# Two q tiles of a head pair share one item, and one pair of banks, in the prompt's attention

## The chip, the cores and the metric

The kernel runs on one core of one Trainium2 chip. The metric is device time in microseconds (us) for one execution, as the median of several runs; lower is better. A profiled execution of the same kernel gives the rows shown below.

## The reference, cut to what matters

The reference is one step of an encoder with two layers (each a mixer and a SwiGLU network, with RMS norms before and after) for 512 prompt frames and 8 running streams of 16 new frames each. The change lies in the attention of the second layer's mixer, and there in the prompt's part: 8 heads of 64 channels, 512 queries and 512 keys, each 64-frame chunk seeing itself and all chunks before it, with a relative-position bias:

```python
scores = einsum('bcqhd,bckhd->bchqk', chunks(q), kb) * 64 ** -0.5 + bias
probs = softmax(where(kpos >= 0, scores, -1e30), axis=-1)
out = einsum('bchqk,bckhd->bqhd', probs, vb)
```

The running streams' attention (the samples) reads 512 cached rows of keys and values for each of the 8 streams.

## The kernel before

All matrix products run on TensorE (PE) with weights split by ScalarE (ACT) and VectorE (DVE) into a coarse and a residual part (`split`, line 228), so that three fast products stand for one. The attention itself is computed in plain fp32.

The program is written by generators that a small planner, `Weave` (lines 48 to 84), takes turns with. The planner keeps a clock of its own: every matrix product adds an estimate (`mm`, line 164: columns divided by 2.4, in ns, four times as much for fp32, over `share` where products run side by side, plus 2 ns; `flip`, line 169, is a transpose on PE for 109 ns). A generator gives back control with `yield x`, which means "not before x nanoseconds from now", or with an event. Of the generators that are due, the one with the lowest priority number goes on, and of equals the one spawned first. The main line of the kernel has priority 9, so it fills what the others leave. The order that results is the program order; the instructions are then placed on the engines in nearly that order, but one whose inputs are reckoned to be late can be passed by a later one that is ready.

In the second layer's mixer, `odd_mixer` (line 933), the main line makes for each pair of heads j (0 to 3) the transposed keys and queries (`kq_proj`, line 1055), in products of 12 at a time: 48 of 256 columns and 48 of 384 columns for a pair. After each pair it signals `kq_ev[j]`. After the fourth pair it signals `room` and goes on with the first output chunk (`out_chunk`, line 437), whose products of 512 columns fill the time while the attention ends.

Three streams run beside it at priority 1 (line 1231). Two of them take items of the prompt from one shared list (line 1221): an item is a pair j and a q tile qt of 128 queries, with n = 128 (qt + 1) keys. An item takes two PSUM banks (one for each head), and does this:

- scores: two products side by side in the two halves of PE's rows (line 1094);
- for each head the bias is added and the maximum taken by DVE, the exponential and its sum made by ACT (lines 1098 to 1107); then DVE normalises the probabilities (line 1112);
- `yield 2200 + 5 * n`, a due time for the softmax;
- qt + 1 transposes for each head, back into the same bank, and a copy by ACT to SBUF (lines 1114 to 1118);
- `yield 600 + 1.5 * n`, then the products with the values into the bank `pos[j]` of the pair (line 1123). The fourth item of a pair splits that bank into an operand tile.

Once the list of the prompt is empty, the two streams take samples like the third one (`sample_stream`, line 1151). A sample loads 2 MB of cached keys and values in four transfers on the SP queue (`load`, line 1142). The first two samples' rows are loaded early; those of samples 2 to 7 go into the tiles of pool `xpool`, seven in all, of which five come free in this stage: four held the mixer's input, and one (`both`, line 921) holds the bias and is freed by the last item's bias additions. Later loads wait for the scores and value products of earlier samples.

The pool of PSUM banks has eight; an output chunk takes two, a pair's result one, each stream two.

Of the kernel before, what the change touches and what calls it, by code (L numbers as in the profile page):

```python
# [10 lines left out]
AF = mybir.ActivationFunctionType  # L11
ALU = mybir.AluOpType
AX = mybir.AxisListType

P = 128
D = 1024
NK = D // P
NP = 512
# [87 lines left out]
def trunk_kernel(  # L106
# [42 lines left out]
    act, dve = Ordered(tc, nc.scalar), Ordered(tc, nc.vector)  # L149
# [14 lines left out]
    def mm(out, lhsT, rhs, start, stop, n, share=1, more=False):  # L164
        fast = lhsT.dtype == F32R
        W.now += PASS * (max(n, 256) if fast else 4 * n / share) + 2
        nc.tensor.matmul(out, lhsT=lhsT, rhs=rhs, start=start, stop=stop, skip_group_check=more)  # L167

    def flip(out, in_):
        W.now += 109  # L170
        nc.tensor.transpose(out=out, in_=in_, identity=ident)  # L171
# [3 lines left out]
    def nm(s):  # L175
        uid[0] += 1
        return f"{s}{uid[0]}"

    def bank(shape=(P, 512)):
        return psp.tile(list(shape), F32, tag="ps", name=nm("ps"))  # L180
# [4 lines left out]
    def t2(shape):  # L185
        return t2p.tile(list(shape), F32, tag="t2", name=nm("t2_"))

    def st(n=1):
        return stp.tile([P, n], F32, tag="st", name=nm("st"))
# [38 lines left out]
    def split(dst, val):  # L228
        act.copy(out=dst[0], in_=val)
        dve.tensor_tensor(out=dst[1], in0=val, in1=dst[0].bitcast(F32), op=ALU.subtract)  # L230
# [202 lines left out]
    def hid_tile():  # L433
        return hidp.tile([P, 2, NT], F32R, tag="hid", name=nm("hid"))
# [466 lines left out]
    def bias_tables():  # L901
        fscr = drp.tile([P, 8, 384], F32, name="fscr")
        for hh in range(2):
            rev = t4([P, 4, 129])
            hs = slice(4 * hh, 4 * hh + 4)
            nc.sync.dma_start(out=rev, in_=rb_rev[0, hs, :].partition_broadcast(P))
            f = x10([P, 4, 384])
            nc.gpsimd.memset(f[:, :, 0:191], 0.0)
            dve.tensor_tensor(
                out=f[:, :, 191:320], in0=rev, in1=rev[:, :, 0:1].broadcast_to([P, 4, 129]), op=ALU.subtract  # L910
            )
            dve.tensor_copy(out=f[:, :, 320:384], in_=f[:, :, 319:320].broadcast_to([P, 4, 64]))
            nc.sync.dma_start(out=fscr[:, hs, :], in_=f)
        a = fscr[:, :, :]

        def skew(h, nh, q, n):
            return bass.AP(
                tensor=a.tensor, offset=a.offset + h * 384 + 127, ap=[[8 * 384 - 1, q], [384, nh], [1, n]]
            )

        both = x10([P, 2, 4, 256])
        bias = []
        for hh in range(2):
            b = both[:, hh]
            nc.sync.dma_start(out=b, in_=skew(4 * hh, 4, P, 256))
            nc.gpsimd.memset(b[0:64, :, 192:256], NEG)
            bias.append(b)
        bias_s = cst.tile([P, 144], F32, name="bias_s")
        for h in range(8):
            nc.sync.dma_start(out=bias_s[h * LS : (h + 1) * LS, :], in_=skew(h, 1, LS, 144)[:, 0, :])  # L930
        return bias, bias_s

    def odd_mixer(X):
# [13 lines left out]
        def vt(t):  # L947
            return vts[:, t, :]
# [81 lines left out]
        bias, bias_s = bias_tables()  # L1030
# [7 lines left out]
        done = [0] * 4  # L1038
# [5 lines left out]
        def row_max(parts):  # L1044
            m = st()
            if len(parts) == 1:
                dve.tensor_reduce(out=m, in_=parts[0], axis=AX.X, op=ALU.max, negate=True)
            else:
                m2 = st(2)
                for i, p in enumerate(parts):  # L1050
                    dve.tensor_reduce(out=m2[:, i : i + 1], in_=p, axis=AX.X, op=ALU.max)
                dve.tensor_reduce(out=m, in_=m2, axis=AX.X, op=ALU.max, negate=True)
            return m
# [29 lines left out]
        def prompt_stream(items):  # L1083


            for j, qt in items:
                yield kq_ev[j]
                kT, qT = kq[j]
                n = (qt + 1) * P
                nb_ = min(n, 256)  # L1090
                ss = [bank() for _ in range(2)]
                for h in range(2):
                    r = slice(64 * h, 64 * h + 64)
                    mm(ss[h][:, :n], qT[r, qt * P : (qt + 1) * P], kT[r, :n], True, True, n, 2)
                prs = []
                for h in range(2):
                    s, hd = ss[h], 2 * j + h
                    dve.tensor_tensor(
                        out=s[:, n - nb_ : n],
                        in0=s[:, n - nb_ : n],  # L1100
                        in1=bias[hd // 4][:, hd % 4, 256 - nb_ :],
                        op=ALU.add,
                    )
                    m = row_max([s[:, :n]])
                    pr = t2([P, NP])
                    sm = st()
                    act.activation(out=pr[:, :n], in_=s[:, :n], func=AF.Exp, bias=m, accum_out=sm)
                    prs.append((pr, sm))
                for pr, sm in prs:
                    ri = st()  # L1110
                    dve.reciprocal(out=ri, in_=sm)
                    dve.tensor_scalar(out=pr[:, :n], in0=pr[:, :n], scalar1=ri, scalar2=None, op0=ALU.mult)
                yield 2200 + 5 * n
                for h in range(2):
                    s, pr = ss[h], prs[h][0]
                    for kt in range(qt + 1):
                        flip(s[:, kt * P : (kt + 1) * P], pr[:, kt * P : (kt + 1) * P])
                    act.copy(out=pr[:, :n], in_=s[:, :n])
                yield 600 + 1.5 * n
                if j not in pos:  # L1120
                    pos[j] = bank()
                po = pos[j]
                for kt in range(qt + 1):
                    for h in range(2):
                        hd = 2 * j + h
                        mm(
                            po[64 * h : 64 * h + 64, qt * P : (qt + 1) * P],
                            vt(kt)[:, hd * 64 : hd * 64 + 64],
                            prs[h][0][:, kt * P : (kt + 1) * P],
                            kt == 0,  # L1130
                            kt == qt,
                            P,
                            2,
                        )
                done[j] += 1
                if done[j] == 4:
                    ct = cat[4 + j] = hid_tile()
                    split((ct[:, 0, :NP], ct[:, 1, :NP]), po)
                    W.signal(prompt_done[j], 2000)
                yield  # L1140
# [77 lines left out]
                    W.signal(sample_done, 500)  # L1218
                yield

        prompt_items = iter([(j, qt) for j in range(4) for qt in range(4)])
        sample_items = iter(range(NB))
        room = Event()

        def stream(i):
            if i < 2:
                yield from prompt_stream(prompt_items)
            yield room
            yield from sample_stream(sample_items)
# [34 lines left out]
    def main():  # L1264
# [39 lines left out]

        yield from ffn(0, X, mid)
        X = yield from odd_mixer(nxt[0])

        def end():
# [101 lines left out]
```

## Time and profile before

| | us |
|---|---|
| median of 3 runs | 1320.69 |
| lowest and highest | 1320.46, 1320.77 |
| profiled execution, its own time | 1320.24 |
| its span, first to last instruction | 1318.5 |
| PE busy | 1294.0 |
| DVE busy | 889.0 |
| ACT busy | 614.0 |

The span is what the profile's rows lie in; 1.7 us of the profiled execution's time lie around it. A busy time is the time in which an engine had an instruction under way; the ends of PE's products are modelled and overlap the next one's start, so that the cost of a block of products is best read as the distance between its start and the start of the next block.

### The profile page before, as it was taken

The numbers are of one execution on the slowest core, as the hardware profiler recorded it, in microseconds if no ns is written. First come the engines' busy times: TensorE is split into PE (matmuls) and PEld (weight loads), VectorE is DVE, ScalarE is ACT, GpSimd is POOL, SyncE is SP. The second block draws the span as 40 slices with busy tenths as digits, with TensorE's granted clock in tenths as the row PEclk, the third lists the DMA queues.
The fourth block names the chain that finished last, engine by engine and source line by source line (L and its number), as shares of the span: only waits on it lengthen the run. The fifth ranks groups of instructions, "written<-read, shape, count | busy, mean of one in ns | idle before, by whom it ended". The sixth has DMA issues, their size and how long they took to land.

```text
span 1318.5 us, 20069 instructions
## 1 busy us (share of the span) xinstructions
PE 1294.0 (98%) x8060; PEld 1178.4 (89%) x8060; DVE 889.0 (67%) x1452; ACT 614.0 (47%) x1130; POOL 54.9 (4%) x107
## 2 busy tenths in 40 slices
PE   6999999999999999999999999999999999999997
PEld 5998989989899998998799885789999898998996
DVE  6985779837576675776736556489557575864766
ACT  5644546535254352454433455366455261551551
POOL 2200101000000000000210000010000000000000
PEclk9999999999999999999999999999999999999999
DMA  7212253212223122126435336532213021230233
GB/s 249 73 65 81 96 200 138 96 48 81 96 73 120 53 77 112 64 84 218 163 120 195 147 143 250 197 128 102 107 64 128 32 98 63 96 115 30 97 128 128
DMA packets 45965, 150.12 MB, mean 114 GB/s; under 512 B 6576, under 2 KB 8496, under 8 KB 45872
## 3 DMA queue, kind: packets, MB, share of 16 engines
q1 hardware_dynamic: 45872, 148.84, 31.2%
q8 instruction: 63, 1.03, 0.3%
q14 instruction: 30, 0.25, 0.1%
HBM read 133.57 MB, written 15.26 MB: 113 GB/s over the span
## 4 chain that ended last, share of the span: by engine, by line
PE 86%; DVE 5%; issue 3%; ACT 2%; DMA 2%; POOL 1%; SPq 0%; DVEq 0%; POOLq 0%; ACTq 0%
PE ps L167 84%; DVE t L99 3%; PE ps L171 1%; DMA xbuf<-t 1%; POOL st L234 1%; ACT t L99 1%; DMA raw<-in_dram 1%; DVE q L99 1%; ACT q L99 1%; DVE x L99 1%; DVE st L99 0%; ACT ps L99 0%; ACT f L99 0%; POOL t L751 0%; SPq L380 0%
## 5 line engine op out<-in xcount | busy, mean ns | idle before, releaser
L167 PE MATMUL ps<-x,q 128*128 128x320 f32 (+2 forms) x4884 | 727.4, 309 | 1.2 <-DVE q L99 0.8
L167 PEld LDWEIGHTS ps<-x,q 128*128 128x128 f32 x4884 | 717.5, 188 | 6.2 <-issue 2.9
L167 PE MATMUL ps<-q,hid 128*128 128x512 f32 x1800 | 417.3, 391 | 0.2 <-DVE hid L99 0.2
L99 ACT CAST q<-raw 128x1024 fp32r<-128x1024 f32 (+1 forms) x278 | 269.7, 977 | 296.8 <-PE ps L167 247.1
L99 DVE TENSOR_TENSOR q<-raw,q 128x1024 fp32r<-128x1024 f32 (+1 forms) x278 | 313.9, 1132 | 134.4 <-ACT q L99 129.3
L167 PEld LDWEIGHTS ps<-q,hid 128*128 128x128 f32 x1800 | 335.5, 188 | 70.9 <-issue 1.7
L99 ACT COPY t<-ps 128x320 f32<-128x320 f32 (+2 forms) x304 | 135.0, 451 | 193.7 <-PE ps L167 173.8
L99 DVE TENSOR_TENSOR t<-ps,t 128x512 f32<-128x512 f32 (+2 forms) x164 | 100.3, 614 | 93.2 <-PE ps L167 93.0
L99 DVE TENSOR_TENSOR raw<-raw 128x512 f32<-128x512 f32 (+1 forms) x141 | 121.9, 866 | 11.6 <-DMA raw<-in_dram 10.0
L99 DVE TENSOR_TENSOR t<-t,t 128x512 f32<-128x512 f32 (+4 forms) x107 | 57.8, 551 | 48.5 <-ACT t L99 46.7
L234 POOL TENSOR_TENSOR st<-st,mhalf 128x1 f32<-128x1 f32 x45 | 31.7, 705 | 1005.9 <-DVE st L99 1001.1
L99 DVE SCALAR_TENSOR_TENSOR t<-t,st,t 128x512 f32<-128x512 f32 (+1 forms) x60 | 54.5, 925 | 16.6 <-POOL st L234 15.1
L99 ACT ACTIVATE t<-t 128x320 f32<-128x320 f32 (+1 forms) x60 | 40.1, 668 | 45.0 <-issue 26.2
L171 PE MATMUL ps<-ident,t 128*128 128x128 f32 x288 | 42.2, 281 | 12.0 <-DVE t L99 9.6
L171 PEld LDWEIGHTS ps<-ident,t 128*128 128x128 f32 x288 | 33.4, 143 | 21.9 <-DVE t L99 9.9
L99 ACT CAST hid<-t 128x320 fp32r<-128x320 f32 (+1 forms) x96 | 45.9, 482 | 11.1 <-DVE t L99 8.9
L99 DVE TENSOR_TENSOR t<-t 128x320 f32<-128x320 f32 (+3 forms) x90 | 48.8, 542 | 1.4
L99 DVE TENSOR_TENSOR hid<-t,hid 128x320 fp32r<-128x320 f32 (+1 forms) x96 | 48.8, 512 | 0.1
L167 PE MATMUL ps<-q,x 128*128 128x512 f32 x192 | 47.6, 402 | 1.2 <-DVE st L99 0.8
L99 ACT ACTIVATE ps<-t 128x512 f32<-128x512 f32 x40 | 24.1, 603 | 50.6 <-DVE t L99 50.6
L167 PEld LDWEIGHTS ps<-q,x 128*128 128x128 f32 x192 | 36.1, 192 | 10.6 <-DVE q L99 2.3
L99 DVE TENSOR_TENSOR t<-t,ps 128x320 f32<-128x320 f32 x47 | 22.9, 487 | 33.2 <-PE ps L167 33.2
(90 smaller groups left out, 497.5 us busy)
## 6 DMA issues: line engine op xcount, KB each, us to landing
raw<-in_dram SPq DMA_DIRECT2D x184, 512.0 KB, 4.1
x<-in_dram SPq DMA_DIRECT2D x24, 512.0 KB, 6.1
t<-in_dram SPq DMA_DIRECT2D x22, 512.0 KB, 5.8
xbuf<-t SPq DMA_DIRECT2D x15, 512.0 KB, 3.4
t<-xbuf SPq DMA_DIRECT2D x15, 512.0 KB, 3.9
out_dram<-t SPq DMA_DIRECT2D x15, 256.0 KB, 2.0
c<-in_dram SPq DMA_DIRECT2D x4, 512.0 KB, 4.2
fscr<-x SPq DMA_DIRECT2D x2, 768.0 KB, 3.3
```

The source lines that it names most:

```text
L99: ins = op(*args, **kw)
L167: nc.tensor.matmul(out, lhsT=lhsT, rhs=rhs, start=start, stop=stop, skip_group_check=more)
L171: nc.tensor.transpose(out=out, in_=in_, identity=ident)
L234: nc.gpsimd.tensor_tensor(out=r, in0=ms, in1=mhalf, op=ALU.pow)
```

## The change

The items of a pair become three: the first and third q tile together, the second, the fourth. The joined item has 128 + 384 = 512 score columns, which fill the bank of each head: the first tile's lie in columns 0 to 127, the third's behind them. Its softmax runs tile by tile, its transposes come in one block of four for each head, one copy of 512 columns replaces the copies of 128 and of 384, and its value products come in one block. The due time of the softmax has 1500 ns more for the joined item.

```diff
@@ -1083,56 +1083,64 @@
-            for j, qt in items:
+            for j, qts in items:
...
-                n = (qt + 1) * P
-                nb_ = min(n, 256)
                 ss = [bank() for _ in range(2)]
-                for h in range(2):
-                    r = slice(64 * h, 64 * h + 64)
-                    mm(ss[h][:, :n], qT[r, qt * P : (qt + 1) * P], kT[r, :n], True, True, n, 2)
...
+                spans = []
+                n = 0
+                for qt in qts:
+                    spans.append((qt, n, (qt + 1) * P))
+                    n += (qt + 1) * P
+                for qt, at, m in spans:
+                    for h in range(2):
+                        r = slice(64 * h, 64 * h + 64)
+                        mm(ss[h][:, at : at + m], qT[r, qt * P : (qt + 1) * P], kT[r, :m], True, True, m, 2)
+                prs = [t2([P, NP]) for _ in range(2)]
+                for qt, at, m in spans:
+                    c = slice(at, at + m)
+                    nb_ = min(m, 256)
+                    sms = []
+                    for h in range(2):
+                        s, pr, hd = ss[h], prs[h], 2 * j + h
+                        dve.tensor_tensor(
+                            out=s[:, at + m - nb_ : at + m],
...
+                        )
+                        mx = row_max([s[:, c]])
+                        sm = st()
+                        act.activation(out=pr[:, c], in_=s[:, c], func=AF.Exp, bias=mx, accum_out=sm)
+                        sms.append(sm)
+                    for pr, sm in zip(prs, sms):
+                        ri = st()
+                        dve.reciprocal(out=ri, in_=sm)
+                        dve.tensor_scalar(out=pr[:, c], in0=pr[:, c], scalar1=ri, scalar2=None, op0=ALU.mult)
-                yield 2200 + 5 * n
...
+                yield 2200 + 5 * n + 1500 * (len(qts) - 1)
+                for s, pr in zip(ss, prs):
+                    for kt in range(n // P):
                         flip(s[:, kt * P : (kt + 1) * P], pr[:, kt * P : (kt + 1) * P])
                     act.copy(out=pr[:, :n], in_=s[:, :n])
                 yield 600 + 1.5 * n
...
+                for qt, at, m in spans:
+                    for kt in range(qt + 1):
+                        for h in range(2):
...
+                                prs[h][:, at + kt * P : at + (kt + 1) * P],
...
-                done[j] += 1
+                done[j] += len(qts)
...
-        prompt_items = iter([(j, qt) for j in range(4) for qt in range(4)])
+        prompt_items = iter([(j, qts) for j in range(4) for qts in ((0, 2), (1,), (3,))])
```

## Rows read from the trace of the kernel before

The rows write the operands by the program's names: `t` in scores and value products are keys, queries or probabilities, `x,q` the key and query products, `q,hid` those of the output chunk, `ident,t` transposes, `c,t` and `x,t` the samples'. An fp32 product is two instructions.

**Rows 1.** The page, its first and fourth parts: busy time of each engine (share of the span, instructions), and the chain of work that ended last, its share by engine.

```profile
PE 1294.0 (98%) x8060; PEld 1178.4 (89%) x8060; DVE 889.0 (67%) x1452; ACT 614.0 (47%) x1130; POOL 54.9 (4%) x107
...
PE 86%; DVE 5%; issue 3%; ACT 2%; DMA 2%; POOL 1%; SPq 0%; DVEq 0%; POOLq 0%; ACTq 0%
```

**Rows 2.** Stretches of the span: from, to, length, then busy time (instructions) of PE, PE's weight loads, DVE, ACT and POOL, PE's granted clock, the share of the transfer engines and GB/s.

```profile
725.00:789.00 64.00, 64.00 (x478) 53.52 (x480) 35.93 (x98) 31.11 (x86) 0.21 (x1) 1.00 0.37 136
789.00:816.00 27.00, 25.70 (x309) 15.83 (x301) 18.55 (x66) 15.10 (x43) 1.17 (x6) 1.00 0.60 223
816.00:836.00 20.00, 17.87 (x225) 11.27 (x216) 9.92 (x45) 6.88 (x22) 0.20 (x1) 1.00 0.98 373
```

**Rows 3.** PE's instructions in order of time over one pair's period: start, duration, line, operation, operands, tile, shape, count.

```profile
736.73 0.88 PE L167 MATMUL ps<-t,x 128*64 128x128 f32 x12
737.53 1.09 PE L171 MATMUL ps<-ident,t 128*128 128x128 f32 x8
738.38 3.11 PE L167 MATMUL ps<-x,q 128*128 128x256 f32 x24
741.42 0.49 PE L167 MATMUL ps<-t 64*128 64x128 f32 x4
741.84 1.09 PE L167 MATMUL ps<-t,x 128*64 128x128 f32 x16
742.87 0.70 PE L167 MATMUL ps<-t 64*128 64x256 f32 x4
743.50 3.14 PE L167 MATMUL ps<-x,q 128*128 128x256 f32 x24
746.48 0.38 PE L171 MATMUL ps<-ident,t 128*128 128x128 f32 x2
746.61 2.33 PE L167 MATMUL ps<-x,q 128*128 128x384 f32 x12
748.87 0.44 PE L167 MATMUL ps<-t,x 128*64 128x128 f32 x4
749.24 0.92 PE L167 MATMUL ps<-t 64*128 64x384 f32 x4
750.09 0.66 PE L171 MATMUL ps<-ident,t 128*128 128x128 f32 x4
...
753.35 1.13 PE L167 MATMUL ps<-t 64*128 64x512 f32 x4
754.41 2.36 PE L167 MATMUL ps<-x,q 128*128 128x384 f32 x12
756.61 0.82 PE L171 MATMUL ps<-ident,t 128*128 128x128 f32 x6
757.18 2.33 PE L167 MATMUL ps<-x,q 128*128 128x384 f32 x12
```

**Rows 4.** The same view of stretches as in Rows 2, for two parts of that period and for the start of the last pair.

```profile
741.40:747.60 6.20, 6.20 (x57) 5.56 (x57) 4.45 (x17) 3.39 (x13) 0.00 (x0) 1.00 0.16 66
747.60:753.60 6.00, 6.00 (x42) 4.61 (x42) 2.96 (x8) 2.66 (x9) 0.00 (x0) 1.00 0.01 3
...
787.20:794.20 7.00, 6.74 (x58) 4.18 (x58) 6.15 (x22) 4.56 (x14) 0.00 (x0) 1.00 1.03 414
```

**Rows 5.** DVE's instructions in order of time; in brackets the idle time before one and what ended it.

```profile
752.94 0.17 DVE L99 RECIPROCAL st<-st 128x1 f32<-128x1 f32 x1 [0.27 <-ACT t L99]
...
754.86 1.22 DVE L99 TENSOR_TENSOR q<-raw,q 128x1024 fp32r<-128x1024 f32 x1
```

**Rows 6.** ACT's instructions in order of time.

```profile
742.73 0.37 ACT L99 ACTIVATE t<-ps,st 128x128 f32<-128x128 f32 x1 [0.83 <-DVE st L99]
```

**Rows 7.** PE's instructions in order of time, from the fourth pair's items to the samples' end; brackets as in Rows 5.

```profile
790.15 0.26 PE L167 MATMUL ps<-x,t 128*32 128x16 f32 x8 [0.27 <-DVE hid L99]
...
794.80 0.66 PE L171 MATMUL ps<-ident,t 128*128 128x128 f32 x4
...
796.39 0.77 PE L171 MATMUL ps<-ident,t 128*128 128x128 f32 x5 [0.47 <-ACT t L99]
...
799.59 1.08 PE L167 MATMUL ps<-c,t 128*32 128x128 f32 x32 [0.56 <-ACT t L99]
...
814.99 1.11 PE L167 MATMUL ps<-x,t 128*32 128x512 f32 x16
...
817.06 1.10 PE L167 MATMUL ps<-x,t 128*32 128x512 f32 x12 [0.69 <-DMA x<-in_dram]
...
819.06 1.05 PE L167 MATMUL ps<-x,t 128*32 128x512 f32 x4
...
829.01 1.30 PE L167 MATMUL ps<-x,t 128*32 128x128 f32 x40 [1.38 <-ACT t L99]
...
832.98 1.05 PE L167 MATMUL ps<-x,t 128*32 128x512 f32 x4
```

**Rows 8.** The SP queue's own waits from 799 to 830 us: which line waited for which engine, us in total, times, longest.

```profile
SPq L1147 <- DVE ps L99: 13.6, 1, 13.6
```

**Rows 9.** The transfers issued by the SP queue in order of time: start, duration of the issues, line, tile and source, count.

```profile
800.95 1.45 SPq L1147 DMA_DIRECT2D x<-in_dram  x2
...
807.42 0.80 SPq L1147 DMA_DIRECT2D x<-in_dram  x2
...
813.74 2.08 SPq L1147 DMA_DIRECT2D x<-in_dram  x4
```

More of the change, by code (lines that the diff above doesn't have):

```diff
@@ L1083, in prompt_stream @@
         def prompt_stream(items):
-            for j, qt in items:
+            for j, qts in items:
                 yield kq_ev[j]
                 kT, qT = kq[j]
-                n = (qt + 1) * P
-                nb_ = min(n, 256)
                 ss = [bank() for _ in range(2)]
-                for h in range(2):
-                    r = slice(64 * h, 64 * h + 64)
-                    mm(ss[h][:, :n], qT[r, qt * P : (qt + 1) * P], kT[r, :n], True, True, n, 2)
[L1095 to L1112, printed above, removed]
-                yield 2200 + 5 * n
-                for h in range(2):
-                    s, pr = ss[h], prs[h][0]
-                    for kt in range(qt + 1):
@@ new lines, in prompt_stream @@
+                spans = []
[16 more added lines that the diff above has]
+                            out=s[:, at + m - nb_ : at + m],
+                            in0=s[:, at + m - nb_ : at + m],
+                            in1=bias[hd // 4][:, hd % 4, 256 - nb_ :],
+                            op=ALU.add,
+                        )
[7 more added lines that the diff above has]
+                        dve.tensor_scalar(out=pr[:, c], in0=pr[:, c], scalar1=ri, scalar2=None, op0=ALU.mult)
@@ L1122, in prompt_stream @@
                 po = pos[j]
[L1123 to L1134, printed above, removed]
-                done[j] += 1
+                for qt, at, m in spans:
+                    for kt in range(qt + 1):
+                        for h in range(2):
+                            hd = 2 * j + h
+                            mm(
+                                po[64 * h : 64 * h + 64, qt * P : (qt + 1) * P],
+                                vt(kt)[:, hd * 64 : hd * 64 + 64],
+                                prs[h][:, at + kt * P : at + (kt + 1) * P],
+                                kt == 0,
+                                kt == qt,
+                                P,
+                                2,
+                            )
+                done[j] += len(qts)
                 if done[j] == 4:
```

## Prediction

> **What bounds the kernel now.** I read the page first, then the waits, then the stretches of the span around the prompt's attention, then TensorE's (PE) instructions in order of time there. The page shows PE busy for 98% of the span, and on 86% of the chain that ended last [rows 1]; VectorE (DVE) and ScalarE (ACT) are far from full. So time can be won only where PE stands idle, or where its products come cheaper. The first three pairs' attention runs in 725 to 789 us, and there PE is busy for 64.00 of 64.00 us: the key and query products fill every gap [rows 2]. Behind it, from 789 to 836 us, the fourth pair and the samples run, and PE stands idle for 1.30 + 2.13 = 3.4 us [rows 2]. Those idle pieces are 0.27 us behind a weight's residue, 0.47 and 0.56 us behind ACT, 0.69 us behind a transfer of cached rows, 1.38 us behind ACT again [rows 7]. In the last 20 us the transfer engines are 98% busy [rows 2], so the samples there run close to the speed of their loads.
>
> **The change, part by part.** The products, transposes, additions, exponentials and normalisations stay the same in number and size. Eight ACT copies fall away (128 + 384 columns become 512, for two heads of four pairs), but ACT is busy for 31.11 of 64 us [rows 2] and only feeds PE: worth nothing by itself. Four softmax pauses and four places in the planner's order go. That leaves three terms.
>
> *Block starts on PE.* A block costs the distance from its start to the next block's [rows 3]. Scores of the first, third and fourth tile: 0.42, 0.85 and 1.06 us; so each 128 columns cost 0.21 us, and a block 0.21 us beside them. Joined scores have 512 columns: 1.06 us if the second tile's weights hide behind the first's products, 1.27 if not; against 1.27 before. I take 1.17, as one weight load of four lies in the open. Value products: 0.37 + 0.80 us become one block of 16 instructions, which costs 1.03: 0.14 less, or nothing. Transposes: 0.13 + 0.57 us become a block of eight, which costs 0.85: 0.15 more, since a short run of transposes between fast products hides part of itself; or no more. Together 0.09 us less for a pair, 0.4 us in four; bounds from 1.4 less (0.35 a pair) to 0.6 more (0.15).
>
> *The softmax's lateness.* The planner's clock gives both orders by hand (256 columns 109 ns, 384 columns 162, a transpose 109). Before: the first tile's transposes are due 2.84 us behind its scores, the third's 4.12 behind its own. After: 2200 + 2560 + 1500 = 6.26 us behind the joint scores. For an inner pair that gives: 12 products of 256 columns; transposes of the pair before, joint scores; 12 products; the earlier pair's value products, scores of the second tile; 24 products; 12 of 384; transposes of the second tile and then of the joint item; 12 products; value products of the second, scores of the fourth, value products of the joint item; 24 products. In PE time, from the start of the joint scores to the second tile's transposes: 1.17 + 1.52 (half of 3.04) + 1.03 + 0.63 + 2.98 + 2.20 = 9.5 us, and 0.4 more to the joint item's [rows 3]. DVE must do in this time what it now does for the first two tiles and one result (4.45 us) and for the third (2.96) [rows 4]: 1.17 + 7.41 + two waits of 0.27 for ACT [rows 5] = 9.1 us. That fits by 0.4 us, so I cost it at nothing in the inner pairs; what hides it are the 48 fast products between. The cover is gone if one of the splits of a weight's residue, 1.22 us on DVE [rows 5], falls into this time: 0.8 us a pair, 2.5 us in three.
>
> The fourth pair is tighter, since sample 0 shares DVE. From 787.20 to 794.20 us DVE has 0.85 us free [rows 4], the second tile's transposes stand at 794.80 us, and sample 0's wait for ACT at 796.39 us as it is [rows 7]. The third tile's 2.96 us now come ahead of both, so they are up to 2.96 - 0.85 = 2.1 us later. The lower bound is no loss: output products stand ready behind them, and 1.3 us of waits is already in this stretch and may be swallowed. I take 0.5 us, nearer the lower bound, since up to 1.3 us of the 2.1 can go into waits that are there already.
>
> *Loads of the samples.* The planner's clock behind the last signal, by hand (an output product 215 ns, a sample's scores 922, its value products 2173), with the end of each block. Before: 12 products 2.6, scores of the first tile 2.8, value products of the pair before 3.7, scores of the second 4.1, of sample 0 5.0, 3 products 5.7, transposes 5.9, 9 products 7.8, first value products and third scores 8.7, transposes of the second and of sample 0 9.7, 3 products 10.3, second value products 10.7, fourth scores 11.6, value products of sample 0 13.8, transposes of the third 14.4, scores of sample 1 15.5, 6 products 16.8, third value products 17.4, scores of sample 2 18.3. After, with the 0.87 us of transposes taken off that before lie ahead of the signal: 6 products and those transposes 1.3, joint scores 2.2, scores of sample 0 3.1, value products of the pair before 3.9, second scores 4.4, 12 products 7.0, transposes of sample 0 7.5, 6 products 8.8, transposes of the second and the joint item 10.1, value products of sample 0 12.3, second value products 12.7, fourth scores 13.6, joint value products 14.4, scores of sample 1 15.4, of sample 2 16.4. So the fourth tile's scores, whose bias additions free the bias tile, come 2.0 us later, sample 2's scores 1.9 sooner, and sample 3's (two blocks of value products and the last prompt item further on) at 24.3 instead of 27.1. On the SP queue the first of the late loads waits 13.6 us for DVE, that is for the bias tile [rows 8], and goes out at 800.95 us; the next at 807.42, when sample 2's keys are free; then four from 813.74, when samples 2 and 3 free theirs [rows 9]. The bias tile comes free about 2 us later, which nothing waits for: its load is needed only by the scores at 814.99 us [rows 7]. The keys of sample 3 come free about 2.8 us sooner, and with them a load of sample 5, for which PE now waits 0.69 us at 817.06, and whose last head pair then runs alone for 1.05 us at 819.06, where all four together take 1.11 [rows 7]. Bounds: nothing, since 20 us of full transfer engines follow in any case, and 0.69 + 1.05 + 1.38 = 3.1 us, with the later wait at 829.01 gone too. I take 0.7 us.
>
> Sum: -0.4 + 0.5 - 0.7 = -0.6 us on the profiled execution's 1320.24, so 1319.6; the median of the runs shown, 1320.69, is 0.45 above that execution, so **1320.1 us**. With all bounds at one side the sum is -4.5 or +0.6 + 2.1 + 2.5 = +5.2 us.
>
> **The rivals.** A difference of 0.2% is 2.64 us, about what a measurement of this kernel can tell from no change.
>
> Loads come early: the third term is at its end, 3.1 us, with 0.4 from the blocks: 1320.7 - 3.5 = 1317.2 us. For it: all three pieces lie in the stretch whose transfer engines are full, behind 5.5 us (808.22 to 813.74) in which no load went out [rows 9]. Against it: the wait at 829.01 is put down to ACT, not to a load.
>
> DVE comes late, the other side: both bounds of the second term, 2.1 + 2.5 us, less 0.4: 1324.9 us. It decides from the point where a weight's split comes ahead of the joint softmax in each inner pair; the last pair alone gives 1322.4, which is within 0.2%. For it: the margin is only 0.4 us. Against it: the split in the row ends at 756.08, 14.7 us behind the first tile's scores, outside the 9.5 us.
>
> One bank, two engines: the first tile's exponential by ACT and the third tile's bias addition by DVE now touch one bank, and would have to take turns. The trace has the exponential of 128 columns at 0.37 us [rows 6]; uncovered, for two heads of four pairs, that is 3.0 us: 1323.7 - 0.4 = 1323.3 us, just the bound of slower. For it: before, each bank had one softmax. Against it: DVE has the other head's addition and maximum meanwhile, and the 0.4 us of margin take part. The Trainium skill (PSUM — Partial Sum Buffer, "PSUM bank collisions raise a hardware error") says that ScalarE and VectorE must be kept apart by semaphores on one bank and quadrant even at different columns; by that rule the turns are taken. No row of before shows it, as no bank there holds two softmaxes.
>
> That the change does nothing to the order is no rival: four items and their due times are gone.
>
> **How the numbers follow.** The forecast, a change within 2.64 us, has 0.61; its own range is 1318.1 to 1323.3. Early loads 0.18, late DVE 0.13, the shared bank 0.05 (on the bound; I count it as slower). In 0.03 the instructions behind the mixer are placed in another order and move it beyond the bound, faster. So faster 0.21, same 0.61, slower 0.18. The range leaves out about one in ten at each side: it reaches down past the early loads' 1317.2 to 1316.9, and up past the shared bank to 1323.7, short of the late DVE's 1324.9.
>
> **What would show it.** In 725 to 789 us PE stays without idle time; the joint scores cost 1.06 to 1.27 us from start to start, sixteen value products 1.03, eight transposes 0.85. No wait of a transpose for DVE in the inner pairs: if it is there, 0.3 us and more each, DVE was late. In the fourth pair a wait of transposes of up to 2 us. On the SP queue the loads that now start at 813.74 us start about 2 us earlier; if they do not, the third term is nothing. DVE's additions for the third tile start behind ACT's exponential of the first in the same bank, or before it. The forecast is wrong if PE's idle time from 789 to 841 us is below 1 or over 6 us, or if the blocks' distances change by more than 0.35 us a pair.

## The result, and the profile after

The changed kernel takes 1323.32 us in the median of 13 runs (1322.23 to 1324.91), the kernel before 1320.70 in 13 runs beside it (1320.28 to 1320.94): a ratio of 1.0022 [1.0013, 1.0030], 0.22% slower. That lies inside the range I gave and outside the forecast of a change within 0.2%. The profiled execution took 1324.31 us, 1.0 above that median, and that of the kernel before 0.5 below its own: the profiles differ by 4.07 us, the medians by 2.62. What follows accounts for the 4.07 us; which part of it is smaller in the median run is not shown.

First and fourth part of the page, as in [rows 1]:

```profile
PE 1297.0 (98%) x8060; PEld 1180.7 (89%) x8060; DVE 888.9 (67%) x1452; ACT 615.3 (47%) x1122; POOL 57.2 (4%) x107
...
PE 81%; DVE 7%; DMA 4%; issue 3%; ACT 3%; POOL 1%; SPq 1%; DVEq 0%; POOLq 0%; ACTq 0%
```

The eight ACT copies are gone (1130 to 1122), nothing else in number; DVE, transfers and ACT have grown on the chain. The three stretches of [rows 2], here of after:

```profile
725.00:789.00 64.00, 63.25 (x463) 53.06 (x465) 36.46 (x101) 31.27 (x82) 0.21 (x1) 1.00 0.34 123
789.00:816.00 27.00, 25.87 (x284) 16.90 (x280) 18.60 (x66) 16.02 (x43) 1.17 (x6) 1.00 0.63 243
816.00:836.00 20.00, 17.21 (x262) 10.75 (x255) 9.48 (x45) 6.88 (x21) 0.20 (x1) 1.00 1.02 386
```

PE's idle time has hardly moved behind 789 us (3.9 for 3.4 us); 0.75 us are new in the stretch from 725 to 789 us. Idle time does not account for the loss, so I cut the time at events that both orders share: the start of the first pair's first scores; the end of its fourth item's transposes; the point where the 96 key and query products that run beside the third pair's items (they are the fourth pair's) and the value products of the third pair's third tile are done (M); the start of the last few value products of the last sample (V); the first norm addition of the output on DVE (N).

| us | before | after | |
|---|---|---|---|
| first scores, from the span's start | 718.96 | 719.33 | +0.37 |
| first pair | 19.42 | 21.39 | +1.97 |
| second and third pair, to M | 44.61 | 44.01 | -0.60 |
| M to V | 56.83 | 56.19 | -0.64 |
| V to N | 13.46 | 16.39 | +2.93 |
| N to the end | 465.3 | 465.3 | 0.0 |

Ahead of the first scores nothing was changed; up to 1.1 us differ there between the profiles of all kernels below. So the loss has two places, the first pair and the end of the last stretch, and between them lie gains of 0.60 and 0.64 us.

**The first pair.** ACT in order of time, before and then after:

```profile
719.46 1.28 ACT L99 ACT_TABLE_LOAD   x1
720.75 0.37 ACT L99 ACTIVATE t<-ps,st 128x128 f32<-128x128 f32 x1
```

```profile
721.26 1.28 ACT L99 ACT_TABLE_LOAD   x1 [1.45 <-DVE st L99]
722.55 0.37 ACT L99 ACTIVATE t<-ps,st 128x128 f32<-128x128 f32 x1
```

Before, the table of the exponential is loaded while DVE makes the first maximum. After, the load itself waits for that maximum, so its 1.28 us come behind the wait. The trace's semaphores show why. Before, and in every profile below whose first pair has four items, the first exponential waits for DVE alone and the load for nothing. After, and in every profile with a joint first item, that exponential waits for DVE and for PE, which writes the third tile's scores into the same bank; where the table is not yet loaded, a wait for DVE then stands ahead of the load too. That the second wait put it there is my reading. DVE has done the second tile's additions by then; the reciprocal of the exponential's sum waits, and the third tile's addition comes behind it, at 723.12 us. PE shows what follows:

```profile
723.04 0.17 DVE L99 RECIPROCAL st<-st 128x1 f32<-128x1 f32 x1 [0.66 <-ACT t L99]
```

```profile
726.97 0.98 PE L171 MATMUL ps<-ident,t 128*128 128x128 f32 x7
728.46 0.52 PE L171 MATMUL ps<-ident,t 128*128 128x128 f32 x3 [0.51 <-ACT t L99]
...
729.82 1.12 PE L167 MATMUL ps<-t 64*128 64x512 f32 x2
730.87 0.65 PE L167 MATMUL ps<-t,x 128*64 128x128 f32 x6
731.45 1.12 PE L167 MATMUL ps<-t 64*128 64x512 f32 x2
```

Transposes wait 0.51 us, and the fourth item's scores, whose two heads run side by side for 1.06 us in [rows 3], go out one head after the other at 1.05 us each.

**An inner pair**, PE as in [rows 3]:

```profile
740.72 3.12 PE L167 MATMUL ps<-x,q 128*128 128x256 f32 x24
743.77 1.14 PE L167 MATMUL ps<-t 64*128 64x128 f32 x8
744.84 1.09 PE L167 MATMUL ps<-t,x 128*64 128x128 f32 x16
745.86 0.70 PE L167 MATMUL ps<-t 64*128 64x256 f32 x4
746.49 5.23 PE L167 MATMUL ps<-x,q 128*128 128x256 f32 x36
751.96 1.56 PE L171 MATMUL ps<-ident,t 128*128 128x128 f32 x12 [0.24 <-ACT t L99]
753.27 2.34 PE L167 MATMUL ps<-x,q 128*128 128x384 f32 x12
755.54 1.09 PE L167 MATMUL ps<-t,x 128*64 128x128 f32 x16
```

The joint scores cost 744.84 - 743.77 = 1.07 us from start to start, sixteen value products 1.02. The view puts the transposes' wait of 0.24 us down to ACT, but ACT had itself waited for DVE, which has no wait in its rows from 746.23 to 752.41 us:

```profile
750.66 0.48 ACT L99 ACTIVATE t<-ps,st 128x256 f32<-128x256 f32 x1 [0.56 <-DVE st L99]
```

So DVE was late here by about 0.2 us. In the third pair no transpose waits. The bank's turns, ACT and then DVE:

```profile
745.73 0.37 ACT L99 ACTIVATE t<-ps,st 128x128 f32<-128x128 f32 x1 [1.43 <-DVE st L99]
```

```profile
746.23 0.43 DVE L99 TENSOR_TENSOR ps<-ps,x 128x256 f32<-128x256 f32 x1
```

DVE's third-tile addition starts 0.13 us behind the end of ACT's exponential in that bank. The Trainium skill (PSUM — Partial Sum Buffer, "PSUM bank collisions raise a hardware error") asks for such turns; the trace agrees. Here PE's products hide them.

**The last stretch.** Stretches from M to V and from V to N, PE's output products alone (first busy time and count), before and after:

```profile
782.99:839.82 56.83, 17.43 (x61) 10.46 (x61) 0.67 (x1) 0.57 (x1) 1.00 0.73 278
839.82:853.28 13.46, 13.17 (x57) 10.84 (x58) 1.67 (x5) 1.60 (x5) 1.00 0.28 82
```

```profile
784.73:840.92 56.19, 13.67 (x48) 8.13 (x48) 0.68 (x1) 0.59 (x1) 1.00 0.74 284
840.92:857.31 16.39, 16.10 (x70) 13.24 (x71) 1.76 (x5) 1.70 (x5) 1.00 0.21 69
```

Of 118 output products, 61 stood among the samples' blocks before, 48 after. The 13 that are left over run at the end, where one costs 13.46 / 57 = 0.236 us: 3.1 us, for a loss of 2.93 from V to N. Yet V itself comes only 0.64 us sooner. By the trace the last load of cached rows lands 49.87 us behind M before and 49.94 after, so the samples' end seems to go by the loads (tested below). What PE did in the meantime instead of 13 products:

```profile
790.22 0.70 PE L167 MATMUL ps<-t 64*128 64x256 f32 x2
...
792.91 0.70 PE L167 MATMUL ps<-t 64*128 64x256 f32 x2
...
827.02 1.05 PE L167 MATMUL ps<-x,t 128*32 128x512 f32 x4 [1.40 <-DMA x<-in_dram]
...
829.70 1.30 PE L167 MATMUL ps<-x,t 128*32 128x128 f32 x40 [0.93 <-ACT t L99]
```

The second tile's scores are split by head (0.63 us twice, once before), and a load is waited for 1.40 us (0.69 in [rows 7]). The rest is seen when each of PE's instructions from M to V is charged with the time to the next one's start, waits apart. Thirteen output products fewer are 3.76 us less. Against them the samples' value products cost 1.53 us more (10.91 for 9.38), the transposes 0.90 (10.28 for 9.38), the waits 0.44 and the rest 0.24, with the same number of each: 3.1 us. The value products come in 13 pieces for 7, since transposes and another sample's scores fall between them. One sample's forty, before and then after:

```profile
809.65 1.08 PE L167 MATMUL ps<-t,t 128*32 128x128 f32 x32
810.55 0.40 PE L167 MATMUL ps<-x,t 128*32 128x128 f32 x8
```

```profile
810.91 0.63 PE L167 MATMUL ps<-t,t 128*32 128x128 f32 x12
811.48 0.77 PE L171 MATMUL ps<-ident,t 128*128 128x128 f32 x5
812.18 0.74 PE L167 MATMUL ps<-t,t 128*32 128x128 f32 x18
```

Whole, they cost 1.23 us from start to start; in two pieces, with ten more instructions behind the last row, 0.57 + 1.00.

### The profile page after: what moved, and what is told of

Its sections match the earlier page's. It is cut to its first block, busy times and chain, and to the rows that moved or that the text cites. A ratio compares the mean times of both kernels' runs of the same rounds, so it can differ in the third digit from the quotient of the medians.

```text
span 1322.6 us, 20046 instructions
## 1 busy us (share of the span) xinstructions
PE 1297.0 (98%) x8060; PEld 1180.7 (89%) x8060; DVE 888.9 (67%) x1452; ACT 615.3 (47%) x1122; POOL 57.2 (4%) x107
## 3 DMA queue, kind: packets, MB, share of 16 engines
q8 instruction: 63, 1.03, 0.3%
## 4 chain that ended last, share of the span: by engine, by line
PE 81%; DVE 7%; DMA 4%; issue 3%; ACT 3%; POOL 1%; SPq 1%; DVEq 0%; POOLq 0%; ACTq 0%
PE ps L167 80%; DVE t L99 4%; ACT t L99 1%; DMA xbuf<-t 1%; PE ps L171 1%; DMA t<-in_dram 1%; DMA raw<-in_dram 1%; POOL st L234 1%; DVE q L99 1%; DVE st L99 1%; DMA x<-in_dram 1%; ACT q L99 1%; DVE x L99 1%; ACT ps L99 0%; DVE ps L99 0%
```

## The experiments

All are compared with the kernel before on the same chip. M, V and N as above; "left" are the output products behind V; the last four columns are of each kernel's profile. In joint_pair1 the fourth item's transposes stand ahead of M; their 0.85 us are counted behind it, as in the others.

| | median us (runs) | ratio [interval] | first pair | M to V | left | V to N |
|---|---|---|---|---|---|---|
| joint_pair0 | 1322.90 (11) | 1.0015 [1.0007, 1.0024] | 21.39 | 56.89 | 57 | 13.47 |
| joint_pair1 | 1325.34 (6) | 1.0030 [1.0018, 1.0042] | 19.45 | 56.55 | 66 | 15.51 |
| joint_pairs12 | 1324.74 (6) | 1.0031 [1.0019, 1.0043] | 19.45 | 56.64 | 76 | 17.68 |
| joint12_due | 1324.08 (11) | 1.0020 [1.0011, 1.0029] | 19.43 | 58.86 | 65 | 15.25 |
| joint_pair3 | 1325.09 (5) | 1.0038 [1.0025, 1.0050] | 19.45 | 57.72 | 64 | 14.96 |
| warm_table | 1321.49 (11) | 1.0006 [0.9998, 1.0015] | 19.76 | 55.23 | 70 | 16.39 |
| warm_before | 1320.86 (11) | 0.9999 [0.9990, 1.0008] | 19.74 | 56.69 | 57 | 13.46 |
| held_before | 1315.73 (3) | 0.9958 [0.9943, 0.9972] | 19.45 | 49.58 | 67 | 15.70 |
| held_after | 1319.28 (8) | 0.9982 [0.9972, 0.9992] | 21.40 | 49.78 | 73 | 17.07 |
| three_before | 1321.32 (11) | 1.0004 [0.9995, 1.0013] | 19.45 | 57.43 | 59 | 13.82 |
| three_after | 1324.02 (7) | 1.0027 [1.0016, 1.0038] | 19.77 | 56.18 | 76 | 17.70 |
| three_pair3 | 1319.01 (11) | 0.9985 [0.9976, 0.9994] | 19.45 | 53.12 | 66 | 15.50 |
| due37_after | 1320.85 (11) | 0.9997 [0.9988, 1.0005] | 21.41 | 54.70 | 64 | 15.02 |
| due29_after | 1325.87 (5) | 1.0040 [1.0028, 1.0053] | 21.41 | 57.00 | 77 | 17.90 |
| due60_before | 1322.61 (11) | 1.0013 [1.0004, 1.0022] | 19.42 | 60.41 | 49 | 11.55 |
| due60_pair3 | 1320.60 (11) | 0.9996 [0.9987, 1.0005] | 19.42 | 59.12 | 49 | 11.55 |
| due47_pair3 | 1321.34 (11) | 1.0005 [0.9997, 1.0014] | 19.42 | 59.02 | 57 | 13.36 |
| warm_due37 | 1319.64 (12) | 0.9986 [0.9978, 0.9995] | 19.77 | 54.19 | 64 | 15.03 |

### Which pair loses: joint_pair0, joint_pairs12, joint_pair3, joint_pair1

```diff
-        prompt_items = iter([(j, qts) for j in range(4) for qts in ((0, 2), (1,), (3,))])
+        joint = (0,)        # (1, 2), (3,), (1,)
+        prompt_items = iter(
+            [(j, qts) for j in range(4) for qts in (((0, 2), (1,), (3,)) if j in joint else ((0,), (1,), (2,), (3,)))]
+        )
```

> Only the first pair of heads has the joined item; the other three pairs keep four items. Theory A: the loss lies in single pairs. In the two profiles the first pair's period (from its first scores to the end of its last transposes) grew from 19.42 to 21.39 us, so this kernel takes about 2.0 us more than before, 1322.7 us, with a spread as small as that of before (0.7 us). Theory B: each joined pair costs the same, so one of four costs 0.65 us: 1321.4 us.

> Only the second and third pair have the joined item. Theory A: the inner pairs gain, 0.60 us in two by the profiles (44.61 to 44.01 us): 1320.1 us, and no idle time of PE between 725 and 789 us. Theory B: each joined pair costs 0.65 us: 1322.0 us.

> Only the fourth pair has the joined item. Theory A: the stretch with the samples loses between 1.0 and 2.3 us, and the changed kernel's wide spread of 2.7 us comes from here, from the samples' loads: 1322.3 us with a spread over 1.5 us. Theory B: 0.65 us more, 1321.4 us, with the spread of before.

> Only the second pair has the joined item. The gain of an inner pair is 0.27 to 0.30 us by three profiles. Theory P: the fourth pair starts from the order of before if the third pair has come back to it; then 1320.4 us. If the order behind the last signal differs, 1322 us and more, in the last stretch alone.

The joint item in the first pair alone gives 21.39 us there, as in after, and leaves the last stretch as it was. In the second and third pair it gains 44.61 - 44.07 = 0.54 us up to M, and then the last stretch, whose items are the four old ones, is 4.0 us longer. So it is not the joint item itself that loses there: joint_pair1, joint_pairs12 and joint_pair3, which hand the streams another order in the last stretch, have more products left, 64 to 76 for 57. Neither of the two theories put down for joint_pairs12 and joint_pair3 had this, and both runs took longer than either said.

### The table: warm_table, warm_before

```diff
         bias, bias_s = bias_tables()
+        warm = st()
+        nc.gpsimd.memset(warm, 0.0)
+        act.activation(out=warm, in_=warm, func=AF.Exp)
```

> The changed kernel, with one exponential of a single column placed on ACT behind the bias tables, ahead of the attention, so that the load of ACT's table (1.28 us at 721.26) is done before the first softmax. Theory A: the first exponential no longer waits for it, and the first pair loses 1.0 to 1.3 us less: 1322.2 us. Rival: the first pair's loss is that of the bank's turns and of PE's split blocks alone; then less than 0.4 us change, 1323.3 us.

> The kernel before with the one-column exponential behind the bias tables, as in warm_table. If that exponential helps the joint item alone, because before the table is loaded ahead of the first maximum anyway, the first pair stays at 19.4 us and the time within 0.1% of before (1319.4 to 1322.0 us). The rival, that the early load of the table is worth its 1.28 us to any order of the items: the first pair falls to 18.0 to 18.5 us, and the time to 1319 to 1319.7 us.

In warm_table ACT has no table load ahead of the first exponential, and PE's fourth scores run side by side again:

```profile
728.16 1.42 PE L171 MATMUL ps<-ident,t 128*128 128x128 f32 x11 [0.46 <-DVE st L99]
...
730.10 1.13 PE L167 MATMUL ps<-t 64*128 64x512 f32 x4
```

The first pair falls by 21.39 - 19.76 = 1.63 of the 1.97 us. The time falls from 1323.32 to 1321.49 us. In the kernel before the same line is worth nothing (19.74 for 19.42 us, ratio 0.9999): there the load was hidden already.

### The loads: held_before, held_after

```diff
+                elif b < 4:
+                    kc, vc = held[b] = load(b, [x10([P, 2, D]) for _ in range(2)])
                 else:
-                    kc, vc = load(b, [x10([P, 2, D]) for _ in range(2)])
+                    kc, vc = held[2 + b % 2]
```

> The kernel before, with the loads of cached rows for samples 4 to 7 left out (8 MB of 12): they use the rows of samples 2 and 3 again, which stay in their tiles. It says what the last stretch (from the end of the third pair's value products of the third tile to the first norm's addition, 70.29 us before) costs without these loads. Theory L (the last stretch waits for loads): shorter by 1.7 us and more, the wait of 0.69 us and the split scores of 1.05 us at 819 us gone. Theory O (it is the order of PE's blocks and the waits for DVE and ACT): within 0.7 us.

> The changed kernel with the same loads left out. The last stretch is 72.58 us in the changed kernel's profile, 2.29 more than before. Theory L: the difference to the kernel before without these loads is under 0.5 us in this stretch, and the spread of the times falls to that of before. Theory O: the difference stays above 1.3 us.

Both kernels leave out the loads of samples 4 to 7. The two windows of output products, held_before and then held_after:

```profile
783.85:833.43 49.58, 14.29 (x51) 8.82 (x51) 0.67 (x1) 0.58 (x1) 1.00 0.39 150
833.43:849.13 15.70, 15.41 (x67) 12.67 (x68) 1.67 (x5) 1.60 (x5) 1.00 0.21 74
```

```profile
785.52:835.30 49.78, 12.65 (x45) 7.65 (x45) 0.68 (x1) 0.58 (x1) 1.00 0.42 152
835.30:852.37 17.07, 16.78 (x73) 13.80 (x74) 1.76 (x5) 1.71 (x5) 1.00 0.20 67
```

Without the late loads V comes 7.3 and 6.4 us sooner: the loads do set it. The two reach V equally late behind M (0.2 us apart), and six products more are left, 6 x 0.235 = 1.4 of the 1.57 us between their last stretches. So the order costs something that no load explains; charged as above, the samples' value products again cost 1.52 us more and the transposes 0.81.

### One due time in pair two: joint12_due

```diff
-                yield 2200 + 5 * n + 1500 * (len(qts) - 1)
+                yield 2200 + 5 * n + 1500 * (len(qts) - 1) - (50 if (j, qts) == (2, (3,)) else 0)
```

> Only the second and third pair have the joined item, and the due time of the third pair's fourth item is 50 ns sooner. By the planner's clock that item's transposes come due 2 ns after the last key and query product and so fall behind the signal for the last pair; 50 ns sooner they stand ahead of it, as before the change. Theory P (the last stretch of joint_pairs12 lost 4.0 us because these transposes fell behind the signal and the order after it changed): the last stretch is back within 0.7 us of 70.3, and the time 1320.1 to 1320.9 us. Rival: the joined items cost in another way, and the last stretch stays above 72.5 us, 1323 us and more.

On the kernel of joint_pairs12, the transposes came ahead of the first output products, as meant (782.69 and 783.48 us). The last stretch stayed long, 74.1 us, of which by an estimate 1.7 belong to a fall of PE's clock (half of its 3.4 us, below); without them it is still 2.1 longer than before. So the 2 ns by which those transposes had been late were not the cause. The order behind them is not that of before: the value products come first and two items' scores follow in one block. That the two streams have changed roles is my reading.

### The bias tile: three_after, three_before, three_pair3

```diff
             if i < 2:
                 yield from prompt_stream(prompt_items)
+            else:
+                yield from prompt_stream(iter([(3, (3,))]))
```

> The kernel of warm_table, and the fourth item of the last pair is taken by the third stream, the one that else takes only samples: its scores stand right behind the joint scores and free the bias tile some 8 to 10 us sooner; sample 0 starts later for it. Theory Q (the last stretch is lost to the bias tile that is freed late, and the loads behind it): the first late load starts at 790 to 796 us instead of 803.10, the stretch from the last pair's products to the first norm addition takes 67.5 to 70.0 us instead of 71.62, and the time is 1317 to 1320 us. Theory O (the order of blocks, and PE's waits for DVE and ACT): the load comes sooner and nothing follows from it; the stretch takes 71 to 74 us, and the time is 1321 to 1324 us.

> The kernel before with four items for each pair, and only the fourth item of the last pair moved to the third stream. Theory Q: the bias tile is freed by the third item instead of the fourth, 2 to 4 us sooner, and the stretch takes 67.5 to 69.5 us instead of 70.29; 1317.5 to 1320 us. Theory O: another order in the last stretch, none of them kinder than that of before: 71 to 74 us, 1321.5 to 1324.5 us.

> Only the last pair has the joint item, as in joint_pair3, and its fourth item is moved to the third stream. The first pair costs what it costs before (19.4 us). Theory Q: the stretch takes 67.5 to 70.0 us instead of 72.68, 1317 to 1320 us. Theory O: 71 to 74 us, 1321.5 to 1324.5 us.

The item (3, (3,)) is taken out of the shared list in the same edit. The first late load went out sooner in all three (at 793.74, 797.03 and 795.83 us), and only three_pair3 gained: there the last load lands 47.9 us behind M instead of 49.9, V follows (53.12 us), and it is faster than both kernels. In three_after the load gained 9 us and the last one landed as late as ever (49.3 us), with 76 products left. A sooner first load alone was worth nothing here.

### What is left at the end: due37_after, due29_after, due60_before, due60_pair3

```diff
-                yield 3300
+                yield 3700        # 2900; 6000
```

> The kernel after, with the due time of a sample's softmax at 3700 ns of the planner's clock instead of 3300; nothing else is changed. In the program's order of TensorE's instructions 54 of the output products of 512 columns then stand ahead of the last sample's last value products, against 48 in after and 61 in before. Theory F (the last stretch is lost because fewer output products stand between the samples' blocks to cover their waits, and so more are left for the end): the stretch from the last pair's products to the first norm addition falls from 72.58 to 71.0 to 72.0 us, and the time to 1321.3 to 1322.5 us. The rival R (the number of covered blocks is a by-product, and the joint item's own place in the last pair costs it): 72.3 to 73.0 us, 1322.8 to 1324.0 us.

> The same with 2900 ns: 41 of the output products stand ahead of the last sample's value products. Theory F: the stretch is 73.5 to 75.0 us, as in the two other orders with 42 (74.32 and 73.88), and the time 1324.3 to 1326 us. The rival R: 72.3 to 73.0 us, 1322.8 to 1324.0 us.

> The kernel before, with four items for each pair, and 6000 ns for a sample's softmax: 69 output products ahead of the last value products instead of 61. Theory F: the stretch falls from 70.29 to 67.5 to 69.3 us, the time to 1317.7 to 1319.7 us. The rival: 70 to 71 us, within 0.1% of before; with later loads 71 us and more.

> The kernel of three_pair3 (the joint item in the last pair alone, its fourth item on the third stream), with 6000 ns for a sample's softmax: 69 output products stand ahead of the last value products, against 52. Theory F: the stretch falls from 68.62 to 65.5 to 67.5 us, the time to 1315.5 to 1318 us. The rival R: 68 to 69.5 us, 1318.3 to 1320 us; or later, if the samples free their tiles later and the loads follow: 70 us and more, 1320 us and more.

The due time of the samples' softmax, a line that the change does not touch, moves the loss both ways. due37_after, then due60_before:

```profile
784.90:839.60 54.70, 15.52 (x54) 9.25 (x54) 0.68 (x1) 0.59 (x1) 1.00 0.78 292
839.60:854.62 15.02, 14.73 (x64) 12.11 (x65) 1.76 (x5) 1.70 (x5) 1.00 0.23 74
```

```profile
783.41:843.82 60.41, 19.01 (x69) 11.96 (x69) 0.67 (x1) 0.58 (x1) 1.00 0.69 262
843.82:855.37 11.55, 11.35 (x49) 9.23 (x50) 1.67 (x5) 1.59 (x5) 1.00 0.29 101
```

With 64 left for 70 M to N is 69.72 us, 2.9 less than in after, a larger fall than I had expected, and the whole loss is gone (0.9997). Half of that is V to N; the other half is M to V, where PE's waits are 1.0 us less and the value products and transposes cost 1.3 less than in after, though six more output products stand there. No run has 3700 with the order of before, so how much of this gain any order would have had is open. With 77 left it is 2.3 longer; about 1.7 of these are the clock (the same estimate), so of this run only V to N (17.90 for 16.39) bears on the question. Upwards there is a limit, and both runs at 6000 missed what the theory said: with 49 left the samples free their tiles later, the last load lands 54.7 us behind M (52.3 in due60_pair3), and V follows it. So N goes with two things: when the last load lands, and how many products are left then. They do not fix it alone: in the profiles without a fall of the clock V comes 5.1 to 7.5 us behind the last landing, depending on the waits and pieces in between.

### Together: warm_due37, due47_pair3

```diff
+        act.activation(out=warm, in_=warm, func=AF.Exp)
...
-                yield 3300
+                yield 3700        # due47_pair3: three_pair3 with 4700, without the first line
```

> The kernel after with both repairs: the one-column exponential of warm_table behind the bias tables, and 3700 ns for a sample's softmax as in due37_after. If the two losses are of their own (the table's load in the first pair, the covered waits in the last stretch), the gains add: 1320.85 - 1.6 (what warm_table took off the first pair) = 1319.2 us, 1318.5 to 1320.0, 0.06 to 0.18% below before; the first pair to the end of the key and query products takes 63.8 to 63.9 us, the last stretch 69.5 to 70.3. The rival: the two shift the same phase, so that one gives back what the other gains: 1320.5 us and more.

> three_pair3 with 4700 ns for a sample's softmax: 61 output products ahead of the last sample's value products, against 52 there and 69 with 6000 ns, where the last loads landed 4 us later and the gain was lost. If the loads stay as early as in three_pair3 (the last landing at 831 to 832.5 us), nine products less are left for the end, 9 x 0.235 = 2.1 us: the time is 1316.5 to 1318 us. If the landing is as late as with 6000 ns (835 us), the last value products end at 841 to 842 us and the time is 1320 to 1321.5 us.

The two repairs nearly add: the joint item with both takes 1319.64 us, 1.2 less than due37_after (1.6 were expected) and 3.7 less than after, and is faster than before by 0.14% [0.05, 0.22]. due47_pair3 has nine products less left and gains nothing, since its last load lands 51.1 us behind M, 3.2 later than in three_pair3; its profile has the clock's fall too.

## Why the prediction was wrong, step by step

*What bounds the kernel.* That PE is the bound held. "Time can be won only where PE stands idle, or where its products come cheaper" left out a third thing: how many of the main line's products stand between the samples' blocks, and how many are left when the last sample is done.

*Block starts.* Right in direction, mis-sized by 0.2 us a pair: -0.09 was taken, -0.30 measured in the second and third pair (44.61 to 44.01 for two), near the low bound of -0.35. Joint scores cost 1.07, the low end, for the 1.17 taken; sixteen value products 1.02 for 1.03; the second tile's four transposes and the joint item's eight, in one block, 1.31, where 0.85 was taken for the eight.

*The softmax's lateness.* In the inner pairs the margin of 0.4 us was too large: in the second pair it was used up and 0.24 us of wait were left, put down to ACT, which had waited for DVE; in the third it held. In the fourth pair DVE is waited for in two places, 0.20 and 0.50 us, against 0.5 taken. The step that failed is that I worked this term out for the inner pairs and the last, and not for the first, which begins at 718.96 us, ahead of the stretch I had read. There it is +1.97 us, of which the table's place is 1.63; the rest (0.34) goes with the wait of 0.46 us for DVE that is left in warm_table.

*Loads of the samples.* The walk through the planner's clock was right in order: behind M the bias tile's load came 1.5 us later (804.20 for 800.95), the next 2.8 sooner (806.35 for 807.42), the next four 0.6 sooner (814.88 for 813.74), where I had said 2 later, 1.9 and 2.8 sooner [rows 9]. SP's loads of after:

```profile
804.20 0.80 SPq L1155 DMA_DIRECT2D x<-in_dram  x2
...
806.35 0.81 SPq L1155 DMA_DIRECT2D x<-in_dram  x2
...
814.88 2.11 SPq L1155 DMA_DIRECT2D x<-in_dram  x4
```

The value was not: the last landing did not move, so the bound of nothing was the right one for the -0.7 taken, and the wait for a load grew from 0.69 to 1.40 us. And the walk that gave those times also told how the output products fall among the blocks; I did not count them on to the last sample. That is the missing term: 13 products, +2.93 us from V to N, with V only 0.64 sooner, since the value products and transposes between cost 2.4 us more in their pieces. The prediction had put the order's effect on them at nothing.

*The rivals.* The shared bank's time, 1323.3 us, is nearly the result, by accident: the turns are taken, and hidden in the inner pairs; in the first pair the shared bank goes with the wait that uncovers the table's load, which is not the price that the rival had. Late DVE came for 0.24 us in one inner pair; early loads did not come.

*The signs I named.* Two of them pointed to it: PE had 0.75 us of idle time from 725 to 789 us, where none was to be, and the four loads came 0.6 us sooner for 2. But PE's idle time from 789 to 841 us (3.9) and the blocks' distances, by which I would have called the forecast wrong, stayed inside the bounds I had set, and it failed all the same.

Still open is why this order of the streams cuts the samples' blocks into more pieces, and why another due time mends it.

## What to carry to other kernels

Where one engine is full and a planner fills it from several streams, a change of one item's length shifts the order of all that follows: count what is left for the end, beside what waits, and try a neighbouring due time before judging the change. Look at the first turn of a loop by itself, for what is done there once (a table load) may lose its cover. A load that goes out sooner was worth nothing here while the last one landed where it did.

## What the runs showed of the hardware

A table load can stand behind the wait of the exponential that needs it: 1.28 us at 721.26, all of it in the open, where before the same 1.28 us were hidden. It did so in the profiles whose first exponential waits for two engines, and not in those where it waits for one. The Trainium skill (ScalarE: Activation LUTs, "Step-by-step: what each stage is for") puts the load right before the activation and its cost at about 2.7 us with the drain; the trace agrees on the place and has 1.28 us, from 719.46 to the exponential's start at 720.75, with no drain beside it.

In three of the profiles (due29_after, joint12_due, due47_pair3) the granted clock fell to 0.50, which is 1.2 GHz, for about 3.4 us, after PE had waited. Stretches of due29_after, all engines, and PE's rows:

```profile
830.00:831.00 1.00, 0.29 (x3) 0.29 (x4) 0.10 (x2) 0.91 (x4) 0.00 (x0) 1.00 1.01 414
831.00:832.00 1.00, 0.47 (x5) 0.23 (x3) 0.56 (x3) 0.55 (x1) 0.00 (x0) 0.80 1.05 430
832.00:833.00 1.00, 0.91 (x20) 0.84 (x24) 0.00 (x0) 0.04 (x1) 0.00 (x0) 0.50 1.02 418
```

```profile
830.71 0.76 PE L171 MATMUL ps<-ident,t 128*128 128x128 f32 x5 [1.33 <-ACT t L99]
832.09 3.62 PE L167 MATMUL ps<-x,t 128*32 128x128 f32 x52 [0.62 <-ACT t L99]
```

The second row holds a sample's forty value products and twelve score products of the next sample. Its first value products start 0.213 us apart for every four at 0.50, where at full clock (after, from 829.70 us) every four are 0.109 apart. Other profiles with waits as long (1.77 us for a load in three_after) kept the clock, so a wait of PE costs itself, and in three of the twenty profiles about 1.7 us more by the estimate above. In the five runs of joint_pair3 the time goes with the granted clock of the whole span (0.999: 1323.21 us; 0.997: 1325.8 in the mean of three; 0.993: 1327.72), which would explain why its median lies above that of after, whose profile is the longer one.
